# Layer 3's up-projection in 15 ktiles as two-by-two blocks with seven products

## The chip, the core and the metric

One NeuronCore of a Trainium2 chip runs one forward step of a four-layer model. The metric is the device time of one execution in microseconds. A core has TensorE (matmuls, PE in the profile, with its weight loads as PEld), VectorE (DVE), ScalarE (ACT), GpSimd (POOL) and SyncE (SP), which run side by side from queues of their own. TensorE multiplies a stationary tile of 128x128 with up to 512 moving columns and writes to PSUM; the other operands lie in SBUF.

## The reference, cut to what matters

Each of the four layers is a token mixer and then a gated ConvFFN. There are 640 tokens (512 of a sample, 128 of a prompt), a width of 1024, and 2816 = 22 x 128 hidden features.

```python
def _conv_ffn(h, w_up, conv_w, conv_b, w_down):
    a, b = jnp.split(h @ w_up, 2, axis=-1)
    ap = jnp.pad(a, ((0, 0), (1, 1), (0, 0)))
    a = ap[:, :-2] * conv_w[0] + ap[:, 1:-1] * conv_w[1] + ap[:, 2:] * conv_w[2] + conv_b
    return (jax.nn.gelu(a) * b) @ w_down
...
        f = (ffn_w_up[i], ffn_conv_w[i], ffn_conv_b[i], ffn_w_down[i])
        x_p = _layer_norm(ALPHA * x_p + m_p[5] * _conv_ffn(h_p, *f), ln_g[i, 1], ln_b[i, 1])
        x_s = _layer_norm(ALPHA * x_s + m_s[5] * _conv_ffn(h_s, *f), ln_g[i, 1], ln_b[i, 1])
```

## The kernel before

Activations are feature-major: a ktile is 128 features on the partitions by 640 tokens. Every float32 operand of a product is split into a high part that TensorE takes as it is and a low part (the rest), and `mm3` (lines 172 to 177) adds three matmuls: high by high, high by low, low by high. `unit` (line 157) loads a piece of weights into a `raw` slot (4 of them), copies the high part on ScalarE (line 163) and subtracts on VectorE (line 164) into a slot of the pool `hlp` (tag `hl`, 6 slots of 8 KB per partition). `split` (line 167) does the same for an activation, which lies in one of 16 slots of `actp`.

The tokens are worked on in two parts, half A of 256 and half B of 384 columns (`HALVES`). In `ffn` (line 560) `up(j)` makes hidden ktile j: two weight units (the convolved branch a and the gate b), each times both halves, over 8 input ktiles; then `ffn_a` copies a into a padded buffer `ap`, and `ffn_g` applies the convolution (lines 512, 514), the gelu (516) and the gate (518, 519) and splits the result. `down` multiplies a chunk of hidden ktiles with the down weights, 8 output ktiles by two halves, and `evac` (436) adds them to x. A chunk's down-projection is issued after the first ktile of the next chunk. The first six ktiles of layer 3 have half A done ahead (`ffn_pre`) and half B in `skew`. Before, the chunks are ktiles 0 to 6, 7 to 13 and 14 to 21; the last one goes through `project`, in which a LayerNorm's steps are issued at fixed positions among the products (`LN_A`).

In layers 0 to 2 VectorE also makes the next layer's modulation (`mod_dve`, line 273) beside the FFN; in layer 3 nothing of that is left, and `bg` does nothing. A scheduler orders each engine's instructions ahead of the run, by program order among those whose operands and slots it expects to be there; each engine then runs its queue in that order and waits at semaphores.

Of the kernel before, what the change touches and what calls it, by code (L numbers as in the profile page):

```python
# [16 lines left out]
D = 1024  # L17
# [16 lines left out]
# half 0 runs ahead of half 1, and 2 of 3 (in front of the pooling, which reads neighbours)  # L34
HALVES = ((0, 256), (256, 640), (0, 384), (384, 640))
HW = 384
# (start, stop, group) with group 0 = sample, 1 = prompt
SEGS = (((0, 256, 0),), ((256, 512, 0), (512, 640, 1)), ((0, 384, 0),), ((384, 512, 0), (512, 640, 1)))
# ktiles of the FFN between its down-projections
FFN_CHUNKS = ((0, 7), (7, 14), (14, 22))  # L40
SKEW = {None: 7, 2: 6, 3: 6, 1: 6, 0: 6}
# units of a projection's weights that half B finds from half A
KEEP = {None: 4, (0, 0): 3, (1, 1): 5, (3, 1): 5, (1, 0): 3, (3, 0): 5}
# layer 0's modulation, blocks of 512 features, in plain float32
MOD32 = (2, 0)
# SKEW ktiles of the FFN run half A ahead of half B, 2 SKEW units of weights: the last SPLIT of them in split parts
# (SPLIT_AHEAD units ahead of their use), of which half B finds the last KEPT; h is split SPLIT_H units from the end
# [17 lines left out]
BAND_KIND = (0, 1, 1, 2, 3)
# tiles of the LN; ktiles that are centred ahead (of the two LNs of a half, and of the last)
# [10 lines left out]
# columns of the packed per-partition vectors  # L77
# [33 lines left out]
class Kern:  # L111
    def __init__(self, ctx, tc, a):
# [4 lines left out]
        self.actp = P("actp", 16)  # L117
        self.hlp = P("hlp", 6)
# [38 lines left out]
    def unit(self, src, shape, e=None):  # L157
        """A piece of weights, split exactly into two float32r parts."""
        nc = self.nc
        r = self.raw(shape)  # L160
        self.load(r, src)
        hl = self.hlp.tile([128, 2] + list(shape[1:]), F32R, tag="hl", name=self.nm("hl"))
        nc.scalar.copy(hl[:, 0], r)  # L163
        (e or nc.vector).tensor_sub(hl[:, 1], r, hl[:, 0])  # L164
        return hl

    def split(self, dst, src, e=None):
        """dst [:, 0] + [:, 1] = src exactly."""
        self.nc.scalar.copy(dst[:, 0], src)  # L169
        (e or self.nc.vector).tensor_sub(dst[:, 1], src, dst[:, 0])  # L170

    def mm3(self, out, lhs, rhs, start, stop):
        """out += lhs^T rhs with (hi, lo) pairs of operands."""
        t = self.nc.tensor
        t.matmul(out, lhs[0], rhs[0], start=start, stop=False)  # L175
        t.matmul(out, lhs[0], rhs[1], start=False, stop=False)  # L176
        t.matmul(out, lhs[1], rhs[0], start=False, stop=stop)  # L177
# [4 lines left out]
    def table(self, f, x):  # L182
        """Has the tables of an activation function loaded ahead of its use, once x is there."""
        self.nc.scalar.activation(self.small("tab", [128, 1]), x.bitcast(F32), f)

    def consts(self):
# [24 lines left out]
        self.cbc = cp.tile([128, 2, D], F32, name="cbc")  # L211
        self.aps = [cp.tile([128, T + 3], F32, name=f"ap{i}") for i in range(2)]
        self.bgq, self.bgf = [], 0.0
        # modulation [part, chunk, ktile, group]
        self.mod = [cp.tile([128, 6, NK, 2], F32, name=f"mod{i}") for i in range(DEPTH)]

    def cond_rows(self):
        """silu(cond) along the free dimension, on every partition."""
# [1181 lines left out]
```

## Time and profile before

| | |
|---|---|
| time, median of 3 runs | 2803.09 us (2801.15 to 2807.25) |
| span of the profiled execution | 2805.7 us |
| layer 3's FFN behind its first LN, to the end | about 2345 to 2806 us |
| TensorE busy | 2749.6 us (98%) |
| VectorE, ScalarE, GpSimd busy | 1973.0, 1240.0, 407.5 us |

The span runs from the first to the last instruction of one profiled execution, whose own time is that span of 2805.7 us; the three runs are timed without a profile. Busy time of TensorE is modelled at its end, since matmuls overlap: a matmul's duration is longer than its distance to the next one. An idle engine costs time only where another one waits for it.

### The profile page before, as it was taken

What the parts mean: (1) busy time and instruction counts of PE and PEld (TensorE: products, weight loads), DVE (VectorE), ACT (ScalarE), POOL (GpSimd) and SP (SyncE); (2) the same over time, 40 slices, a digit from 0 to 9 for tenths busy, and PEclk for the clock granted to TensorE, in tenths of its full rate; (3) what the DMA queues carried; (4) which work ended last, traced back from release to release, by engine and by line L of the source; (5) the groups of instructions that cost most, each with busy time, mean ns of one, the idle gap of its engine ahead of it and who ended that gap; (6) DMA issues with size and microseconds to landing.
All of it is one profiled execution on the core that took longest, in us unless ns stands there. A gap on an engine that the chain in (4) does not pass through costs nothing.

```text
span 2805.7 us, 46039 instructions
## 1 busy us (share of the span) xinstructions
PE 2749.6 (98%) x17826; PEld 2636.0 (94%) x17826; DVE 1973.0 (70%) x4263; ACT 1240.0 (44%) x2286; POOL 407.5 (15%) x417
## 2 busy tenths in 40 slices
PE   7999999999999999999999999999999999999998
PEld 4799999999989999999978999999799999999998
DVE  6879977857697887777587878775756558534344
ACT  5656232336496752323367423234532248423233
POOL 1250000024303300000442000005100042000003
PEclk9999999999999999999989999999999999999999
DMA  7735644432402445455104554542422224322221
GB/s 241 259 109 163 198 154 149 156 121 80 134 22 83 136 153 158 149 157 153 56 35 150 151 165 151 158 136 80 161 65 91 68 62 152 97 82 68 83 75 54
DMA packets 99932, 344.70 MB, mean 123 GB/s; under 512 B 11392, under 2 KB 14080, under 8 KB 99584
## 3 DMA queue, kind: packets, MB, share of 16 engines
q1 hardware_dynamic: 99712, 341.74, 38.7%
q8 instruction: 141, 2.31, 0.3%
q14 instruction: 79, 0.65, 0.1%
HBM read 336.19 MB, written 2.88 MB: 121 GB/s over the span
## 4 chain that ended last, share of the span: by engine, by line
PE 88%; DVE 5%; issue 2%; ACT 2%; DMA 2%; POOL 1%; POOLq 0%; ACTq 0%; SPq 0%; DVEq 0%
PE mm L175 26%; PE mm L176 26%; PE mm L177 26%; PE mm L487 2%; PE st L352 1%; PE mm L1157 1%; DVE hl L164 1%; DVE tmp L339 1%; DMA raw<-in_wmod 1%; PE mm L1247 1%; PE bc L372 1%; DVE lnt L383 1%; DVE act L170 0%; PE mm L1072 0%; DMA raw<-in_wup 0%
## 5 line engine op out<-in xcount | busy, mean ns | idle before, releaser
L177 PE MATMUL mm<-act,hl 128*128 128x384 f32 (+2 forms) x4928 | 1528.5, 310 | 3.2 <-DVE hl L164 3.2
L175 PE MATMUL mm<-act,hl 128*128 128x384 f32 (+2 forms) x4928 | 1531.5, 311 | 0.0
L176 PE MATMUL mm<-act,hl 128*128 128x384 f32 (+2 forms) x4928 | 1528.6, 310 | 1.2 <-POOL act L418 1.2
L177 PEld LDWEIGHTS mm<-act,hl 128*128 128x128 f32 x4928 | 935.1, 190 | 5.0 <-DVE hl L164 4.4
L176 PEld LDWEIGHTS mm<-act,hl 128*128 128x128 f32 x4928 | 935.9, 190 | 3.7 <-POOL act L418 1.8
L175 PEld LDWEIGHTS mm<-act,hl 128*128 128x128 f32 x4928 | 935.2, 190 | 3.2 <-ACT hl L163 0.6
L163 ACT CAST hl<-raw 128x1024 fp32r<-128x1024 f32 (+1 forms) x433 | 444.1, 1030 | 625.9 <-PE mm L177 560.1
L164 DVE TENSOR_TENSOR hl<-raw,hl 128x1024 fp32r<-128x1024 f32 (+1 forms) x428 | 526.0, 1231 | 67.4 <-ACT hl L163 65.1
L283 DVE SCALAR_TENSOR_TENSOR bc<-raw,cbc 128x512 f32<-128x512 f32 x608 | 406.2, 719 | 130.3 <-DMA raw<-in_wmod 130.0
L436 DVE SCALAR_TENSOR_TENSOR x<-mm,mod,x 128x256 f32<-128x256 f32 (+2 forms) x408 | 166.0, 434 | 200.4 <-PE mm L177 199.8
L514 DVE SCALAR_TENSOR_TENSOR tmp<-ap,vecs,tmp 128x512 f32<-128x512 f32 x352 | 170.5, 547 | 147.6 <-ACT tmp L512 147.4
L333 POOL TENSOR_TENSOR tmp<-x,tmp 128x256 f32<-128x256 f32 (+1 forms) x180 | 178.0, 993 | 153.2 <-DVE x L436 109.0
L527 POOL MEMSET ap<- 128x1 f32 x24 | 2.1, 99 | 1188.4 <-DVE tmp L514 735.3
L502 ACT COPY ap<-mm 128x256 f32<-128x256 f32 x88 | 33.0, 375 | 265.2 <-PE mm L177 265.2
L333 POOL TENSOR_TENSOR tmp<-x 128x256 f32<-128x256 f32 (+1 forms) x30 | 30.7, 1024 | 733.3 <-DVE x L436 694.5
L383 DVE TENSOR_TENSOR lnt<-x,bc 128x256 f32<-128x256 f32 (+1 forms) x240 | 109.6, 479 | 14.9 <-PE bc L372 14.4
L332 ACT ACTIVATE lnt<-x 128x256 f32<-128x256 f32 (+1 forms) x112 | 51.2, 467 | 133.3 <-DVE x L436 130.9
L516 ACT ACTIVATE tmp<-tmp 128x640 f32<-128x640 f32 x88 | 65.2, 740 | 100.4 <-DVE tmp L514 100.4
L169 ACT CAST act<-tmp 128x640 fp32r<-128x640 f32 x117 | 84.9, 726 | 52.1 <-DVE tmp L519 31.8
L512 ACT ACTIVATE tmp<-ap,vecs 128x512 f32<-128x512 f32 (+1 forms) x176 | 106.4, 658 | 0.0
L339 DVE TENSOR_TENSOR tmp<-tmp,lnt 128x384 f32<-128x384 f32 (+1 forms) x126 | 93.7, 745 | 14.1 <-ACT lnt L332 12.6
L487 PE MATMUL mm<-h,raw 128*128 128x256 f32 x416 | 101.2, 399 | 1.8 <-DVE lnt L404 1.8
(209 smaller groups left out, 2684.1 us busy)
## 6 DMA issues: line engine op xcount, KB each, us to landing
raw<-in_wup SPq DMA_DIRECT2D x216, 512.0 KB, 3.5
raw<-in_wmod SPq DMA_DIRECT2D x184, 512.0 KB, 3.5
raw<-in_wdn SPq DMA_DIRECT2D x64, 448.0 KB, 3.4
raw<-in_wdn SPq DMA_DIRECT2D x46, 512.0 KB, 3.6
raw<-in_wgv SPq DMA_DIRECT2D x24, 512.0 KB, 4.1
raw<-in_wgo SPq DMA_DIRECT2D x19, 512.0 KB, 3.9
raw<-in_wqk SPq DMA_DIRECT2D x18, 512.0 KB, 3.5
raw<-in_wgu SPq DMA_DIRECT2D x16, 512.0 KB, 3.5
```

The source lines that it names most:

```text
L163: nc.scalar.copy(hl[:, 0], r)
L164: (e or nc.vector).tensor_sub(hl[:, 1], r, hl[:, 0])
L175: t.matmul(out, lhs[0], rhs[0], start=start, stop=False)
L176: t.matmul(out, lhs[0], rhs[1], start=False, stop=False)
L177: t.matmul(out, lhs[1], rhs[0], start=False, stop=stop)
L283: nc.vector.scalar_tensor_tensor(out=self.bc(), in0=r[:, sl], scalar=1.0, in1=self.cbc[:, g, sl], op0=ALU.mult, op1=ALU.mult, accum_out=ac ...
L333: nc.gpsimd.tensor_add(S.s[0], z, S.s[0] if n > 1 else S.first)
L339: (self.nc.gpsimd if S.pool else self.nc.vector).tensor_add(S.s[1], S.s[1], S.last)
L383: self.nc.vector.tensor_sub(t, self.x[:, k, a:b], MU)
L436: nc.vector.scalar_tensor_tensor(out=self.x[:, m, s0:s1], in0=ps[:, s0 - a:s1 - a], scalar=sc, in1=self.x[:, m, s0:s1], op0=ALU.mult, op1= ...
L487: self.nc.tensor.matmul(ps, w[:, k, :], h32[:, k, :], start=k == 0, stop=k == NK - 1)
L514: nc.vector.scalar_tensor_tensor(out=c[:, sl], in0=ap[:, o + i:o + i + n], scalar=cw(i), in1=c[:, sl], op0=ALU.mult, op1=ALU.add)
```

## The change

For ktiles 7 to 21 of layer 3, `up` is replaced by `up7`. The two weight tiles a and b, each cut into input ktiles 0 to 3 and 4 to 7, are a block matrix of two by two, and h, cut into the same input halves and two halves of 320 tokens, is another. Their product is made from seven block products in place of eight, from sums and differences of blocks. The sums of weights are made on VectorE for every ktile (`S`); the sums of h are made once, in `seven_pre`, in steps beside the first chunk's down-projection, some of them in place of blocks of h. The sums of products are made through copies of PSUM on ScalarE and additions on VectorE, while X and Z go on accumulating. The gate comes with its sign changed, so `ffn_g` gets a form with -1. The low part of the unsummed weights (`wA`) is made by a negated copy on ScalarE and a DMA from GpSimd that adds the raw weights to it.

Layer 3's chunks become 0 to 5, 6 to 10, 11 to 14 and 15 to 21. `actp` has 18 slots, `hlp` 7, of which the conditioning rows `cbc` hold one until layer 2's FFN is done; GpSimd's scratch for DMAs is set to 4096 bytes, which makes room for these. Comments were removed.

```diff
-FFN_CHUNKS = ((0, 7), (7, 14), (14, 22))
+FFN_CHUNKS = {None: ((0, 7), (7, 14), (14, 22)), 3: ((0, 6), (6, 11), (11, 15), (15, 22))}
+SEVEN = {None: NJ, 3: 7}
+HT = T // 2
...
-        self.actp = P("actp", 16)
-        self.hlp = P("hlp", 6)
+        self.actp = P("actp", 18)
+        self.hlp = P("hlp", 7)
...
+    def halves(self, hl, r, e=None, dma=False):
+        nc = self.nc
         nc.scalar.copy(hl[:, 0], r)
-        (e or nc.vector).tensor_sub(hl[:, 1], r, hl[:, 0])
-        return hl
+        if dma:
+            nc.scalar.activation(hl[:, 1], r, AF.Copy, scale=-1.0)
+            nc.gpsimd.dma_start(hl[:, 1].bitcast(F32), r, accum_op=ALU.add)
+        else:
+            (e or nc.vector).tensor_sub(hl[:, 1], r, hl[:, 0])
...
-        self.cbc = cp.tile([128, 2, D], F32, name="cbc")
+        self.cbc = self.hlp.tile([128, 2, D], F32, tag="hl", name="cbc")
...
-    def ffn_g(self, L, j, ap, bA, bB):
+    def ffn_g(self, L, j, ap, bA, bB, neg=False):
...
+        if neg:
+            c = self.tmp([128, T + 1])
+            nc.scalar.activation(c, ap[:, 0:T + 1], AF.Identity, scale=cw(0), bias=self.vec(V_CB + L * NJ + j))
+            for i in (1, 2):
+                nc.vector.scalar_tensor_tensor(out=c, in0=ap[:, i:i + T + 1], scalar=cw(i), in1=c, op0=ALU.mult, op1=ALU.add)
+            nc.scalar.activation(c, c, AF.Gelu_apprx_tanh)
+            g = self.tmp([128, T])
+            for x, y, ps in ((0, 0, bA), (HT, HT, bB[:, 0:512 - HT]), (512, 513, bB[:, 512 - HT:HT])):
+                w = ps.shape[1]
+                nc.vector.scalar_tensor_tensor(out=g[:, x:x + w], in0=ps, scalar=-1.0, in1=c[:, y:y + w],
+                                               op0=ALU.mult, op1=ALU.mult)
+            o = self.act()
+            self.split(o, g)
+            return o
...
                     self.evac(ps, L, 5, m, half)
                     self.bg(at(BG, L))
+                steps(beside, 1)
+
+        def seven_pre():
+            acts = [self.act([128, 2, 2, HT]) for _ in range(3)]
...
+            for k in range(4):
+                if k < 2:
+                    room = [acts[k][:, 0], acts[k][:, 1], acts[2][:, k]]
+                else:
+                    t = self.hlp.tile([128, 3, 2, HT], F32R, tag="hl", name=self.nm("op"))
+                    room = [t[:, i] for i in range(3)]
+                up, lo = fl(hs[k][:, :, :]), fl(hs[k + 4][:, :, :])
+                w, z = self.tmp([128, 2, HT]), self.tmp([128, 2, HT])
+                v.tensor_sub(w, up[:, :, A], up[:, :, B])
+                v.tensor_add(w[:, 0], w[:, 0], w[:, 1])
+                self.split(room[0], w[:, 0])
+                v.tensor_sub(z, lo[:, :, B], up[:, :, B])
+                v.tensor_add(z[:, 0], z[:, 0], z[:, 1])
+                self.split(room[1], z[:, 0])
+                yield
+                v.scalar_tensor_tensor(out=z[:, 0], in0=z[:, 0], scalar=-1.0, in1=up[:, 0, A], op0=ALU.mult, op1=ALU.subtract)
+                v.tensor_sub(z[:, 0], z[:, 0], up[:, 1, A])
+                self.split(room[2], z[:, 0])
+                v.scalar_tensor_tensor(out=z[:, 0], in0=z[:, 0], scalar=-1.0, in1=lo[:, 0, A], op0=ALU.mult, op1=ALU.subtract)
+                v.tensor_sub(z[:, 0], z[:, 0], lo[:, 1, A])
+                self.split(hs[k][:, :, B], z[:, 0])
...
+        def up7(j, ops):
+            v = nc.vector
+            ra, rb = self.raw_unit(a["wup"][L, 2 * j]), self.raw_unit(a["wup"][L, 2 * j + 1])
+            new = lambda n=8: self.hlp.tile([128, 2, n, 128], F32R, tag="hl", name=self.nm("hl"))
+            a1, a2, b1, b2 = ra[:, 0:4], ra[:, 4:8], rb[:, 0:4], rb[:, 4:8]
+            S = self.hlp.tile([128, 16, 128], F32, tag="hl", name=self.nm("sums"))
+            v.tensor_add(S[:, 4:8], b1, b2)
+            v.tensor_add(S[:, 0:4], a1, b1)
+            v.tensor_add(S[:, 8:12], a1, S[:, 4:8])
+            v.tensor_add(S[:, 12:16], a2, S[:, 8:12])
+            wA, wB, wC, wD = new(), new(), new(), new(4)
+            self.halves(wA, ra, dma=True)
+            self.halves(wB, S[:, 8:16])
+            self.halves(wC, S[:, 0:8])
+            self.halves(wD, b2)
+            X, Y, Z = self.mm([128, HT]), self.mm([128, HT]), self.bc([128, HT])
+            def prod(ps, w, k0, rhs, first):
+                for k in range(4):
+                    self.mm3(ps, (w[:, 0, k0 + k], w[:, 1, k0 + k]), rhs[k], first and k == 0, k == 3, not first)
+            def keep(ps):
+                t = self.small("lnt", [128, HT], LNT)
+                nc.scalar.copy(t, ps)
+                return t
+            ap = self.aps[j % 2]
+            prod(X, wA, 0, ops[0], True)
+            r1 = keep(X)
+            prod(Y, wA, 4, ops[1], True)
+            v.tensor_add(ap[:, 1:1 + HT], r1, Y)
+            prod(X, wB, 0, ops[2], False)
+            r2 = keep(X)
+            prod(Z, wC, 4, ops[3], True)
+            m5 = keep(Z)
+            prod(X, wC, 0, ops[4], False)
+            v.tensor_add(m5, m5, X)
+            prod(Z, wB, 4, ops[5], False)
+            v.tensor_add(ap[:, 1 + HT:513], r2[:, 0:512 - HT], Z[:, 0:512 - HT])
+            v.tensor_add(ap[:, 514:642], r2[:, 512 - HT:HT], Z[:, 512 - HT:HT])
+            prod(X, wD, 0, ops[6], False)
+            gs[j] = self.ffn_g(L, j, ap, X, m5, neg=True)
...
-        for ci, (k0, k1) in enumerate(FFN_CHUNKS):
+        for ci, (k0, k1) in enumerate(at(FFN_CHUNKS, L)):
...
-                up(j)
+                if j >= at(SEVEN, L):
+                    up7(j, ops)
+                else:
+                    up(j)
...
-                    down(*pend, False)
+                    pre7 = seven_pre() if j + 1 == at(SEVEN, L) else iter(())
+                    down(*pend, False, pre7)
+                    ops = next(pre7, ops)
...
-    nc = _bacc.Bacc("TRN2", target_bir_lowering=False, num_devices=1)
+    nc = _bacc.Bacc("TRN2", target_bir_lowering=False, num_devices=1,
+                    dynamic_dma_scratch_size=4096)
```

## Rows read from the trace of the kernel before

**Rows 1.** Page, parts 1 and 2: busy us by engine, granted clock by slices.
```profile
PE 2749.6 (98%) x17826; PEld 2636.0 (94%) x17826; DVE 1973.0 (70%) x4263; ACT 1240.0 (44%) x2286; POOL 407.5 (15%) x417
...
PEclk9999999999999999999989999999999999999999
```

**Rows 2.** Windows: length, then PE, PEld, DVE, ACT, POOL busy; clock, DMA share, GB/s.
```profile
2561.35:2575.42 14.07, 14.07 (x98) 14.07 (x97) 5.66 (x9) 5.15 (x10) 0.00 (x0) 1.00 0.24 67
...
2587.50:2636.00 48.50, 48.50 (x333) 48.50 (x332) 19.28 (x32) 7.96 (x10) 0.00 (x0) 1.00 0.27 88
```

**Rows 3.** TensorE's waits, 2345 us to the end: total us, times, longest.
```profile
PE mm L177 <- DVE hl L164: 1.7, 1, 1.7
PE bc L372 <- POOL lnv L360: 1.6, 2, 1.4
PE st L352 <- POOL tmp L333: 1.6, 1, 1.6
```

**Rows 4.** Timeline of TensorE in one ktile: start us, duration us, instruction.
```profile
2561.03 0.28 PE L177 MATMUL mm<-act,hl 128*128 128x256 f32 x1
2561.15 0.34 PE L175 MATMUL mm<-act,hl 128*128 128x384 f32 x1
...
2565.14 0.33 PE L177 MATMUL mm<-act,hl 128*128 128x384 f32 x1
2565.32 0.28 PE L175 MATMUL mm<-act,hl 128*128 128x256 f32 x1
...
2568.06 0.28 PE L177 MATMUL mm<-act,hl 128*128 128x256 f32 x1
```

**Rows 5.** Timeline of TensorE in layer 1's scores: first and last of six.
```profile
852.78 0.31 PE L175 MATMUL mm<-act,act 128*128 128x320 f32 x1
...
853.51 0.31 PE L177 MATMUL mm<-act,act 128*128 128x320 f32 x1
```

**Rows 6.** VectorE by form, 2410 to 2735 us: busy us, mean ns | idle before.
```profile
L164 DVE TENSOR_TENSOR hl<-raw,hl 128x1024 fp32r<-128x1024 f32 x33 | 40.4, 1223 | 9.4 <-ACT hl L163 9.4
L514 DVE SCALAR_TENSOR_TENSOR tmp<-ap,vecs,tmp 128x512 f32<-128x512 f32 x32 | 24.0, 749 | 86.9 <-ACT tmp L512 86.9
...
L170 DVE TENSOR_TENSOR act<-tmp,act 128x640 fp32r<-128x640 f32 x16 | 13.1, 819 | 0.0
L514 DVE SCALAR_TENSOR_TENSOR tmp<-ap,vecs,tmp 128x128 f32<-128x128 f32 x32 | 11.1, 347 | 0.0
```

**Rows 7.** Timeline of VectorE: one ktile's four convolution steps.
```profile
2566.80 1.94 DVE L514 SCALAR_TENSOR_TENSOR tmp<-ap,vecs,tmp 128x512 f32<-128x512 f32 x4 [5.52 <-ACT tmp L512]
```

**Rows 8.** ScalarE by form, the same stretch and columns as rows 6.
```profile
L163 ACT CAST hl<-raw 128x1024 fp32r<-128x1024 f32 x34 | 35.6, 1046 | 94.8 <-PE mm L177 94.8
...
L169 ACT CAST act<-tmp 128x640 fp32r<-128x640 f32 x16 | 11.6, 723 | 0.0
...
L502 ACT COPY ap<-mm 128x256 f32<-128x256 f32 x16 | 6.0, 374 | 60.6 <-PE mm L177 60.6
```

**Rows 9.** DMA issues, whole span: KB each, median us from issue to landing.
```profile
raw<-in_wup SPq DMA_DIRECT2D x216, 512.0 KB, 3.5
...
x<-in_xT SPq DMA_DIRECT2D x1, 2560.0 KB, 9.9
```

**Rows 10.** Timelines of VectorE and GpSimd in the last project.
```profile
2739.56 1.23 DVE L164 TENSOR_TENSOR hl<-raw,hl 128x1024 fp32r<-128x1024 f32 x1 [0.47 <-ACT hl L163]
...
2743.71 1.78 DVE L164 TENSOR_TENSOR hl<-raw,hl 128x1024 fp32r<-128x1024 f32 x1 [0.47 <-ACT hl L163]
...
2744.37 1.99 POOL L339 TENSOR_TENSOR tmp<-tmp,lnt 128x384 f32<-128x384 f32 x1
```

**Rows 11.** TensorE's waits on split weights, whole span: total us, times, longest.
```profile
PE mm L177 <- DVE hl L164: 3.2, 4, 1.7
PE mm L176 <- DVE hl L164: 2.8, 2, 1.7
```

**Rows 12.** Timeline of ScalarE behind the product of rows 4's first line.
```profile
2561.35 0.38 ACT L500 COPY ap<-mm 128x256 f32<-128x256 f32 x1 [1.30 <-PE mm L177]
```

More of the change, by code (lines that the diff above doesn't have):

```diff
@@ L155, in load, with unit @@
         self.nc.sync.dma_start(dst, src)
-    def unit(self, src, shape, e=None):
+    def unit(self, src, shape, e=None, dma=False):
         nc = self.nc
@@ L162, in unit @@
         hl = self.hlp.tile([128, 2] + list(shape[1:]), F32R, tag="hl", name=self.nm("hl"))
+        self.halves(hl, r, e, dma)
+        return hl
+    def halves(self, hl, r, e=None, dma=False):
+        nc = self.nc
         nc.scalar.copy(hl[:, 0], r)
-        (e or nc.vector).tensor_sub(hl[:, 1], r, hl[:, 0])
-        return hl
+        if dma:
[3 more added lines that the diff above has]
+            (e or nc.vector).tensor_sub(hl[:, 1], r, hl[:, 0])
     def split(self, dst, src, e=None):
@@ L170, in split, with mm3 @@
         (e or self.nc.vector).tensor_sub(dst[:, 1], src, dst[:, 0])
-    def mm3(self, out, lhs, rhs, start, stop):
+    def mm3(self, out, lhs, rhs, start, stop, on=False):
         t = self.nc.tensor
-        t.matmul(out, lhs[0], rhs[0], start=start, stop=False)
-        t.matmul(out, lhs[0], rhs[1], start=False, stop=False)
-        t.matmul(out, lhs[1], rhs[0], start=False, stop=stop)
+        t.matmul(out, lhs[0], rhs[0], start=start, stop=False, skip_group_check=on)
+        t.matmul(out, lhs[0], rhs[1], start=False, stop=False, skip_group_check=on)
+        t.matmul(out, lhs[1], rhs[0], start=False, stop=stop, skip_group_check=on)
     def vec(self, col, n=1):
@@ L210, in consts @@
         nc.vector.tensor_sub(self.condr[:, :, 2:4], self.cond, self.condr[:, :, 0:2])
-        self.cbc = cp.tile([128, 2, D], F32, name="cbc")
+        self.cbc = self.hlp.tile([128, 2, D], F32, tag="hl", name="cbc")
+        nc.vector.memset(self.cbc[:, 0, 0:2], 0.0)
         self.aps = [cp.tile([128, T + 3], F32, name=f"ap{i}") for i in range(2)]
@@ L598, in down_unit, with down @@
             return f
-        def down(k0, k1, last):
+        def down(k0, k1, last, beside=iter(())):
             us = down_unit(k0, k1)
@@ L614, in down @@
                     self.bg(at(BG, L))
+                steps(beside, 1)
+        def seven_pre():
+            acts = [self.act([128, 2, 2, HT]) for _ in range(3)]
+            n1, n2, t3 = [], [], []
+            v = nc.vector
+            fl = lambda x: x.bitcast(F32)
+            A, B = slice(0, HT), slice(HT, T)
+            for k in range(4):
[19 more added lines that the diff above has]
+                self.split(hs[k][:, :, B], z[:, 0])
+                for o, r in zip((n1, t3, n2), room):
+                    o.append(r)
+                yield
+            b = lambda k, sl: (hs[k][:, 0, sl], hs[k][:, 1, sl])
+            pair = lambda t: (t[:, 0], t[:, 1])
+            yield ([b(k, slice(0, HT)) for k in range(4)], [b(k + 4, slice(0, HT)) for k in range(4)],
+                   [pair(t) for t in n2], [pair(t) for t in n1], [pair(t) for t in t3],
+                   [b(k + 4, slice(HT, T)) for k in range(4)], [b(k, slice(HT, T)) for k in range(4)])
@@ new lines, in up7 @@
+        def up7(j, ops):
+            v = nc.vector
+            ra, rb = self.raw_unit(a["wup"][L, 2 * j]), self.raw_unit(a["wup"][L, 2 * j + 1])
[24 more added lines that the diff above has]
+            v.tensor_add(ap[:, 1:1 + HT], r1, Y)
+            self.bg(at(BG, L))
+            prod(X, wB, 0, ops[2], False)
+            r2 = keep(X)
+            prod(Z, wC, 4, ops[3], True)
+            m5 = keep(Z)
+            self.bg(at(BG, L))
+            prod(X, wC, 0, ops[4], False)
[3 more added lines that the diff above has]
+            v.tensor_add(ap[:, 514:642], r2[:, 512 - HT:HT], Z[:, 512 - HT:HT])
+            self.bg(at(BG, L))
+            prod(X, wD, 0, ops[6], False)
+            self.bg(at(BG, L))
+            gs[j] = self.ffn_g(L, j, ap, X, m5, neg=True)
@@ L616, in ffn @@
         if L == 0:
             self.bgq.append(self.mod_dve(0, 40, 48))
+        ops = None
         pend = None
-        for ci, (k0, k1) in enumerate(FFN_CHUNKS):
+        for ci, (k0, k1) in enumerate(at(FFN_CHUNKS, L)):
             if ci == 0:
```

## The prediction

> **What bounds the kernel now.** I read the page's first two parts first. TensorE is busy 98% of the span, VectorE 70%, ScalarE 44%, and the granted clock stands at 9 tenths or more in nearly every slice [rows 1]. Then a table by stretches of layer 3's FFN: one ktile of the up-projection takes 14.07 us, a chunk of seven ktiles of the down-projection fills the 48.5 us shown beside it, and in both TensorE is busy for the whole stretch at clock 1.00, the full level of 2.4 GHz, while VectorE works 5.66 of 14.07 us and ScalarE 5.15 [rows 2]. Third, the list of TensorE's waits from 2345 us on: one wait of 1.7 us for split weights at the start, and the LN's waits near the end; the steady part has none [rows 3]. So in this stage time is the number of matmuls times their spacing, and an instruction on another engine costs nothing until it makes TensorE wait.
>
> **What is removed.** Spacing, start to start, is what counts, not the duration of 0.28 or 0.33 us, since matmuls overlap. From the first to the last of 24 matmuls of 384 columns are 3.99 us, of 256 columns 2.74 us; divided by 23 that is 0.173 and 0.119 us [rows 4]. An up-projection ktile has two weight tiles by two parts of the tokens by 8 input ktiles by 3 matmuls: 48 of each width, 48 x 0.173 + 48 x 0.119 = 14.0 us, which is the measured 14.07. The new ktile has seven products of 4 input ktiles by 3 matmuls, 84 in all, with 320 columns each. That width exists in layer 1's scores, where six starts in a row span 0.73 us, 0.146 each [rows 5]; 84 x 0.1465 = 12.31 us. So 1.76 us are saved per ktile, and for 15 ktiles **26.4 us**. The other chunk borders change neither number nor width of the down-projection's matmuls. Chunks of 6, 5, 4 and 7 in place of 7, 7 and 8 add eight weight units and 16 accumulations with their evacuation; TensorE pays nothing for them, and VectorE is idle for over half of a down stretch (19.28 of 48.5 us busy) [rows 2].
>
> **VectorE per new ktile.** From the rows of the stretch by form [rows 6], between whose sizes the cost grows by 1.05 ns a column: four sums of weights at 512 columns, 0.685 us each by the line through 640 (0.819) and 1024 (1.223), 2.74; three low parts of 1024, 1024 and 512 columns, 3.13; four sums of products, 1.6; two convolution steps of 641 columns, 1.77; three gate products, 1.31; the low part of g, 0.82. Together 11.4 us in 17 instructions. Back to back they overlap: four convolution steps whose durations add up to 2.19 us take 1.94 us [rows 6, 7], 0.085 us less per instruction, so 17 of them occupy about 9.9 of 12.31 us. That fits, at 81%, but the slack of the old ktile is gone. ScalarE: four copies and one negated copy of weights (4.5 x 1.05 us), three copies of products (0.43 each), convolution start, gelu and the copy of g, about 8.4 us [rows 8]; that fits easily.
>
> **Slots.** There are 7 slots for split weights; two hold operands from now on, so five are left, and one ktile uses five (sums, A, B, C, D). Ktile j+1 finds its slots as j lets go of them. With t = 0 at the first product of j and 1.76 us a product: A is free at 3.5, C at 8.8, B at 10.5, D at 12.3. New B takes C's slot and is wanted 15.8 after t = 0, new C takes B's and is wanted at 17.6; a cast (1.05), a subtraction (1.22) and some waiting leave 3 to 4 us. New D has 8 us. Only new A is tight: slot free at 3.7, casts and the copies that ScalarE owes in between (A's high part, the copy of the preceding g, a product's copy, the negated copy: 1.05 + 0.72 + 0.43 + 1.1) end at 7.0, then GpSimd issues the accumulating DMA, and the third matmul at 12.6 wants its result. So the DMA is hidden if issue to landing takes up to **5.5 us**.
>
> **The accumulating DMA** is an operation that the trace doesn't show. A plain load of the same 512 KB lands in 3.5 us and one of 2560 KB in 9.9 [rows 9]; so each 512 KB beyond the first costs 1.6 us. An accumulation must read its target too, twice the bytes: 3.5 + 1.6 = 5.1 us, nearest to the first row, and I take that: hidden, **0 us**. The bounds are 3.5 (no more than a load) and 9.9 us, by the far row; at the latter 4.4 us would be missing in each of the 12 ktiles that follow directly on another one (those at 7, 12 and 16 follow on a down-projection, whose units of 3.5 to 5 us leave longer leads), or 53 us.
>
> The Trainium skill (DMA: Bandwidth & Descriptors, "Anatomy of one DMA — SWDGE (gpsimd) path") gives about 2.0 us plus bytes at 436 GB/s for a DMA issued by GpSimd, an estimate of 3.2 us for one pass of 512 KB and 4.4 us with the target read as well. By it the DMA is hidden with a us to spare and the sum stays the same; no run here shows such a DMA yet.
>
> **Handoffs within a ktile.** X and Z gather several products, so the third, fifth, sixth and seventh product must each wait until a copy or a sum has read the bank. One product of 1.76 us covers each. In today's rows ScalarE starts 0.04 us after a product's end, which lies 0.16 us behind the next one's start [rows 4, 12]. Behind a running cast of 1.05 us a copy of 0.43 is done at 1.7 us: just inside. On VectorE a running subtraction of 1.22 us and a sum of 0.48 give 1.8 to 1.9 us, 0.1 too late. Bounds for 60 handoffs: 0, and 0.1 each, 6 us; I take **2 us**, since only one handoff of four is VectorE's and it rarely meets a fresh subtraction.
>
> **The operands, made beside the first down-projection.** Per input ktile 12 VectorE instructions (two of 640 columns, ten of 320), 6.6 us, for four 26.4; the eight weight units of 6 ktiles and the evacuations add 8 x 2.2 us. That makes 44 us, some 37 with the overlap above, in 8 x 5.27 = 42 us of TensorE work. It fits if nothing else comes; the first new ktile's sums and low parts come too (6 us). Bounds 0 and 6 us; I take **2 us**. The steps are queued on VectorE ahead of later weight splits, so those would be what TensorE waits for.
>
> **The tail.** The last project has 7 instead of 8 ktiles, so half B's 22.9 us become 20.0 and LN steps at fixed positions come earlier. There TensorE already waits 1.6 us for GpSimd's sums and up to 1.4 for its power [rows 3]. Position 8 comes 0.36 us earlier, position 23 another 0.67. Bounds 0 and 1.5; I take **1 us**.
>
> **Layers 0 to 2** get 18 instead of 16 activation slots; the six weight slots are the same ones until layer 2 is done, since the conditioning rows occupy the seventh. TensorE's waits on split weights come to 3.2 and 2.8 us over the whole span [rows 11]; about half of that could go or come again: I take 0, bounds -3 and +3.
>
> **Sum.** -26.4 + 0 + 2 + 2 + 0 + 1 = -21.4 us. The profiled execution has a span of 2805.7 us, 2.6 us over the median of 2803.09 and inside the runs' spread, so differences carry over: 2803.1 - 21.4 = **2781.7 us**. With all costs at their low ends 2803.1 - 26.4 - 3 = 2774; with the highs except the DMA's, 2793.
>
> **Rivals.**
> *The DMA paces (slower).* If the landing takes L us over 5.5, each of 12 ktiles waits L - 5.5. With 5 us of other costs the gain is gone at L = 5.5 + 21.4/12 = 7.3 us, which lies between the two load rows. At 8.5 us: 2803.1 - 26.4 + 36 + 5 = 2818 us. For it: descriptors made by GpSimd in software and a read-modify-write, neither of which is in the trace; DMA rows of this stretch already show two loads per ktile. Against it: the queues are a quarter busy there [rows 2]. Chance 0.14.
>
> *VectorE paces.* While GpSimd reads SBUF, a VectorE subtraction of two SBUF operands took 1.78 instead of 1.23 us [rows 10]. If the eight sums and low parts of a ktile (6.7 us) all ran at that rate, 3.0 us would be added: 9.9 becomes 12.9, 0.6 us over the pace in 15 ktiles, 9 us: 2791 us; with the overlap gone too, 14.4 us, 2803.1 - 26.4 + 31 + 5 = 2813. Against it: GpSimd has no arithmetic in this stretch [rows 2], only the DMA's issue. Chance 0.10.
> The Trainium skill (SBUF — State Buffer, "Who interferes with whom") says that a VectorE instruction with two SBUF inputs contends only with GpSimd instructions that read SBUF, not with those that only write. Rows 10 agree on the first half; by the second this rival would cost nothing.
>
> *It doesn't do what it says.* The issue order is fixed ahead of the run. If the copies of products stand one cast too far back, a handoff takes 0.16 + 0.04 + 2.1 + 0.43 = 2.7 us, 1 us too long; one such handoff per ktile costs 15 us (2797 us with the other terms), two cost 30 (2812). Against it: in today's stretch copies start 0.04 us after their product [rows 12]. Chance 0.10.
>
> **Numbers.** The forecast, 2774 to 2793, has 0.66. Of the rivals, the DMA's 0.14 is nearly all slower (0.12, and 0.02 about the same); VectorE's 0.10 splits into 0.06 faster, 0.03 same, 0.01 slower; the order's into 0.02, 0.03 and 0.05. About 0.2%, 5.6 us, is what a measurement of this kernel can tell from no change. So faster 0.74, same 0.08, slower 0.18. The range reaches from 2773 to 2806: it takes in the likeliest case and the milder half of the rivals, and leaves out little below and 0.17 above.
>
> **What would show it.** Right: starts of 320-column matmuls 0.146 us apart, ktiles 12.3 us apart, TensorE busy over the whole of the stretch. Each term has its place: a wait of the third matmul of a ktile on a GpSimd DMA is the first rival; a wait at the first matmul of the third, fifth, sixth or seventh product on ScalarE or VectorE is the handoff; VectorE over 95% busy is the second rival; waits in the first down stretch are the operands'. The forecast is wrong if the landing exceeds 7 us, or if TensorE's idle time in the stretch adds up to more than 20 us.

## The result and the profile after

| | before | changed |
|---|---|---|
| time, median of 4 runs each | 2804.27 us | 2783.05 us (2779.24 to 2784.92) |
| ratio, 95% interval | | 0.9922 [0.9908, 0.9936] |
| span of the profiled execution | 2805.7 us | 2779.9 us |

The change makes the kernel 0.8% faster. A second comparison of the same kernel, run with the experiments below, gave 0.9925 [0.9912, 0.9937].

The page of the changed kernel, where it answers to rows 1: TensorE has 180 matmuls fewer (15 ktiles, 84 in place of 96) and 26.8 us less to do, VectorE and ScalarE have more, and there is a DMA queue that GpSimd feeds (the last line, from the list of DMA issues: KB each, median us from issue to landing).

```profile
span 2779.9 us, 46012 instructions
...
PE 2722.8 (98%) x17646; PEld 2607.5 (94%) x17646; DVE 2063.7 (74%) x4464; ACT 1289.5 (46%) x2340; POOL 419.3 (15%) x432
...
hl<-raw POOLq DMA_DIRECT2D x15, 512.0 KB, 4.5
```

The windows that answer to rows 2 (same columns): all five ktiles of the first run of new ktiles, then two of them alone. Each lasts 12.32 us instead of 14.07, TensorE is busy without a break at clock 1.00, and VectorE works 10.1 us, ScalarE 8.1 us of it.

```profile
2466.53:2528.12 61.59, 61.59 (x422) 61.59 (x421) 45.87 (x78) 37.38 (x52) 3.47 (x4) 1.00 0.43 110
2491.16:2503.48 12.32, 12.32 (x87) 12.32 (x85) 10.10 (x18) 8.10 (x12) 0.86 (x1) 1.00 0.48 129
2503.48:2515.80 12.32, 12.32 (x87) 12.32 (x85) 10.11 (x18) 8.09 (x12) 0.86 (x1) 1.00 0.41 97
```

The list of TensorE's waits from ktile 6 to the end, as in rows 3 (total us, times, longest). In 15 new ktiles and three down-projections nothing is waited for; what is left are the LN's waits, 1.9 where 1.6 was, and one of 0.2 us in the last project.

```profile
PE st L366 <- POOL tmp L347: 1.9, 1, 1.9
PE bc L386 <- POOL lnv L374: 1.4, 1, 1.4
PE bc L386 <- DVE lnv L370: 0.3, 1, 0.3
PE mm L187 <- ACT act L181: 0.2, 1, 0.2
```

Layer 3's part can be measured by itself. ScalarE's copy of ktile 6's first product is the last landmark that both kernels share. First the line of before, then that of the changed kernel, from ScalarE's timelines:

```profile
2413.71 0.38 ACT L500 COPY ap<-mm 128x256 f32<-128x256 f32 x1 [1.29 <-PE mm L177]
```

```profile
2413.39 0.38 ACT L514 COPY ap<-mm 128x256 f32<-128x256 f32 x1 [1.40 <-PE mm L189]
```

From there to the end of the span are 2805.7 - 2413.7 = 392.0 us before and 2779.9 - 2413.4 = 366.5 us after. I call this the **stage**; it became **25.5 us** shorter, and it is compared in every experiment, since the same stage of the changed kernel run again came to 366.4 us, within 0.1.

### The profile page after: what moved, and what is told of

It reads as the page before. It is cut to its first block, busy times and chain, and to the rows that moved or that the text cites. A ratio compares the mean times of both kernels' runs of the same rounds, so it can differ in the third digit from the quotient of the medians.

```text
span 2779.9 us, 46012 instructions
## 1 busy us (share of the span) xinstructions
PE 2722.8 (98%) x17646; PEld 2607.5 (94%) x17646; DVE 2063.7 (74%) x4464; ACT 1289.5 (46%) x2340; POOL 419.3 (15%) x432
## 4 chain that ended last, share of the span: by engine, by line
PE 87%; DVE 5%; ACT 3%; DMA 2%; issue 2%; POOL 1%; SPq 0%; POOLq 0%; ACTq 0%; DVEq 0%
PE mm L187 26%; PE mm L188 26%; PE mm L189 26%; PE mm L501 2%; PE st L366 1%; DVE hl L177 1%; DVE tmp L353 1%; DMA raw<-in_wmod 1%; ACT x L410 1%; PE mm L1370 1%; PE bc L188 1%; PE bc L189 1%; PE bc L187 1%; ACT hl L172 1%; DVE lnt L409 1%
## 5 line engine op out<-in xcount | busy, mean ns | idle before, releaser
L187 PE MATMUL mm<-act,hl 128*128 128x384 f32 (+3 forms) x4688 | 1455.7, 311 | 0.9 <-ACT act L431 0.7
L189 PE MATMUL mm<-act,hl 128*128 128x384 f32 (+3 forms) x4688 | 1453.2, 310 | 2.3 <-DVE hl L177 2.1
L188 PE MATMUL mm<-act,hl 128*128 128x384 f32 (+3 forms) x4688 | 1453.1, 310 | 2.4 <-POOL act L432 1.5
L188 PEld LDWEIGHTS mm<-act,hl 128*128 128x128 f32 x4688 | 888.3, 189 | 5.0 <-POOL act L432 2.5
L187 PEld LDWEIGHTS mm<-act,hl 128*128 128x128 f32 x4688 | 887.5, 189 | 4.5 <-ACT act L431 0.9
L189 PEld LDWEIGHTS mm<-act,hl 128*128 128x128 f32 x4688 | 887.5, 189 | 4.1 <-DVE hl L177 3.7
L172 ACT CAST hl<-raw 128x1024 fp32r<-128x1024 f32 (+4 forms) x441 | 438.9, 1001 | 517.9 <-PE mm L189 427.7
L177 DVE TENSOR_TENSOR hl<-raw,hl 128x1024 fp32r<-128x1024 f32 (+4 forms) x421 | 499.6, 1190 | 55.4 <-ACT hl L172 52.9
L450 DVE SCALAR_TENSOR_TENSOR x<-mm,mod,x 128x256 f32<-128x256 f32 (+2 forms) x432 | 175.9, 435 | 159.9 <-PE mm L189 159.1
L543 DVE SCALAR_TENSOR_TENSOR tmp<-ap,vecs,tmp 128x512 f32<-128x512 f32 (+1 forms) x292 | 141.6, 547 | 59.9 <-ACT tmp L541 59.6
L181 ACT CAST act<-tmp 128x640 fp32r<-128x640 f32 (+1 forms) x127 | 89.2, 705 | 68.5 <-DVE tmp L548 36.5
L182 DVE TENSOR_TENSOR act<-tmp,act 128x640 fp32r<-128x640 f32 (+1 forms) x127 | 100.7, 794 | 7.9 <-ACT act L181 7.7
L353 DVE TENSOR_TENSOR tmp<-tmp,lnt 128x384 f32<-128x384 f32 (+1 forms) x126 | 93.5, 744 | 13.8 <-ACT lnt L346 12.3
L545 ACT ACTIVATE tmp<-tmp 128x640 f32<-128x640 f32 x73 | 54.1, 741 | 105.5 <-DVE tmp L543 105.4
L410 ACT ACTIVATE x<-lnt,vecs 128x256 f32<-128x256 f32 (+1 forms) x128 | 82.4, 649 | 27.6 <-DVE lnt L409 26.8
```

Source lines behind the costliest of these rows:

```text
L187: t.matmul(out, lhs[0], rhs[0], start=start, stop=False, skip_group_check=on)
L188: t.matmul(out, lhs[0], rhs[1], start=False, stop=False, skip_group_check=on)
L189: t.matmul(out, lhs[1], rhs[0], start=False, stop=stop, skip_group_check=on)
L353: (self.nc.gpsimd if S.pool else self.nc.vector).tensor_add(S.s[1], S.s[1], S.last)
L410: nc.scalar.activation(z, t, AF.Identity, scale=scale, bias=bias)
L450: nc.vector.scalar_tensor_tensor(out=self.x[:, m, s0:s1], in0=ps[:, s0 - a:s1 - a], scalar=sc, in1=self.x[:, m, s0:s1], op0=ALU.mult, op1= ...
```

## The experiments

All of them start from the changed kernel. "Stage" is the stretch above, 366.5 us in the changed kernel. In two_dmas, six_slots, keep_thrice and vector_over the scheduler also orders TensorE's matmuls otherwise: in 12, 12, 12 and 9 of the 15 new ktiles a few matmuls of a later product stand ahead of those that wait. In the other kernels with 15 new ktiles their order is that of the changed kernel.

| kernel | time, us | ratio to before, 95% interval | stage, us |
|---|---|---|---|
| again | 2783.61 | 0.9925 [0.9912, 0.9937] | 366.4 |
| no_seven | 2804.53 | 0.9998 [0.9990, 1.0007] | 392.1 |
| ten_ktiles | 2790.70 | 0.9948 [0.9933, 0.9963] | 375.2 |
| two_dmas | 2868.14 | 1.0231 [1.0215, 1.0246] | 449.0 |
| low_on_vector | 2782.15 | 0.9921 [0.9907, 0.9934] | 366.7 |
| six_slots | 2826.83 | 1.0081 [1.0064, 1.0098] | 412.7 |
| keep_thrice | 2785.99 | 0.9932 [0.9917, 0.9947] | 372.8 |
| ops_after | 2782.23 | 0.9918 [0.9901, 0.9934] | 366.4 |
| vector_full | 2781.79 | 0.9916 [0.9899, 0.9932] | 367.4 |
| vector_over | 2788.29 | 0.9937 [0.9923, 0.9952] | 374.3 |
| sum_on_gpsimd | 2789.24 | 0.9943 [0.9928, 0.9958] | 373.7 |

### Is it the number of matmuls? (again, no_seven, ten_ktiles)

The changed kernel once more, for a narrower interval and a second trace:

> The changed kernel as it is, to narrow the gain. Hidden-work theory (all that the change adds lies beside TensorE's matmuls, the gain is 15 ktiles times 14.07 - 12.32 = 26.2 us, less about 0.7 us at the end): 25 us under the kernel before, a ratio of 0.991. If the gain is really the 21.2 us of the first medians, 4 us are lost somewhere that the profiled execution didn't show: ratio 0.9925.

The chunks, slots and scratch of the change, but no ktile with seven products:

```diff
-SEVEN = {None: NJ, 3: 7}
+SEVEN = {None: NJ}
```

> Ktiles 7 to 21 go through the old up-projection again; chunk borders, 18 and 7 slots and the conditioning rows' place stay as changed. Hidden-work theory: the seven products are the whole gain, so this kernel has the old time, span 2805 us within 3, ktiles 14.07 us apart. Rival (the slots and chunks bring part of the gain, by fewer waits in layers 0 to 3): span 2800 us or less.

Seven products in 10 instead of 15 ktiles:

```diff
-SEVEN = {None: NJ, 3: 7}
+SEVEN = {None: NJ, 3: 12}
```

> Only ktiles 12 to 21 are made by seven products; the operands are then made beside the second down-projection (5 ktiles, 8 x 4.39 = 35 us of TensorE, against some 36 us of VectorE work). Hidden-work theory: the gain is 1.75 us per ktile, so five ktiles fewer cost 8.8 us, span 2789 us, plus 0 to 6 us where the operands don't fit beside the shorter chunk. Rival (a fixed part of the gain, not proportional to the ktiles): span 2780 to 2784 us.

Without the seven products the kernel is at the time of before (0.9998), and the stage at 392.1 us: the other chunk borders, the 18 activation slots, the seventh weight slot and the smaller scratch are together worth nothing that the measurement can tell. With 10 such ktiles the stage is 375.2 us, 8.7 us more than with 15: 8.7 / 5 = 1.74 us a ktile, where the windows give 14.07 - 12.32 = 1.75. So the gain is linear in the number of ktiles.

### Is the accumulating DMA hidden, and how far? (two_dmas, low_on_vector, six_slots)

A second accumulating DMA behind the first. The copy is taken times -2, and what is too much is added back, so the result stays the low part:

```diff
-            nc.scalar.activation(hl[:, 1], r, AF.Copy, scale=-1.0)
+            nc.scalar.activation(hl[:, 1], r, AF.Copy, scale=-2.0)
             nc.gpsimd.dma_start(hl[:, 1].bitcast(F32), r, accum_op=ALU.add)
+            nc.gpsimd.dma_start(hl[:, 1].bitcast(F32), hl[:, 0].bitcast(F32), accum_op=ALU.add)
```

> The copy is scaled by -2, and a second accumulating DMA of the same size, chained behind the first, adds the high part: the same low part, twice the landing. DMA theory (A's low part is due at the third matmul of the next ktile, 2.1 us after today's landing): the second landing comes 4.5 us later, TensorE waits about 2.5 us at the third matmul of 12 ktiles, 30 us, span 2810 us; none at ktiles 7, 12 and 16, which follow on a down-projection. Rival (there is much more room than 2.1 us): span 2780 us.

The kernel became slower than before. The stage grew by 82.5 us. GpSimd's timeline of one ktile, and then the page's rows on the two DMAs (KB each, median us to landing):

```profile
2468.97 0.87 POOL L175 DMA_DIRECT2D hl<-raw  x1 [13.31 <-ACT hl L174]
2474.34 0.86 POOL L176 DMA_DIRECT2D hl<-hl  x1 [4.50 <-DMA hl<-raw]
```

```profile
hl<-raw POOLq DMA_DIRECT2D x15, 512.0 KB, 4.6
hl<-hl POOLq DMA_DIRECT2D x15, 512.0 KB, 6.4
```

The second is issued 5.4 us after the first and lands 6.4 us later: 11.8 us from the first issue. TensorE's waits, and then the windows of the same ktile (columns as in rows 2): the wait, the matmuls behind it, and what follows.

```profile
PE mm L190 <- DMA hl<-hl: 54.3, 14, 5.5
```

```profile
2475.56:2480.74 5.18, 0.31 (x4) 0.05 (x2) 3.85 (x6) 0.62 (x2) 0.00 (x0) 0.92 0.98 274
2480.74:2486.77 6.03, 6.03 (x23) 6.03 (x23) 0.99 (x4) 1.06 (x2) 0.00 (x0) 0.50 0.05 20
2486.77:2495.72 8.95, 8.95 (x63) 8.95 (x62) 5.53 (x9) 6.24 (x8) 1.72 (x2) 1.00 0.40 78
```

It is the third matmul of the ktile, in the order of the program, that waits, as the DMA rival said. Of the ktiles behind a down-projection, which I expected to be spared, only 7 was; 12 waited 0.5 and 16 waited 2.9 us. The cost has two parts: the waits, 54.3 us in 14 ktiles, and the time behind them. In the second window 23 matmuls take 6.03 us, 0.262 each where 0.1465 is the rule, at a granted clock of 0.50, which is the lower of the two levels (1.2 GHz); ahead of it two starts lie 5.2 us apart, so TensorE had stood for 5.0 us. Over the stage the slower starts make up the rest of the 82.5 us, some 28 us. It is more than was expected by both: the second landing takes 6.4 us where the first takes 4.6, and the waits have this price behind them.

The low part of `wA` on VectorE, as for the other weights, without negated copy and DMA:

```diff
-            self.halves(wA, ra, dma=True)
+            self.halves(wA, ra)
```

> The low part of the unsummed weights is a VectorE subtraction instead of ScalarE's negated copy and GpSimd's DMA. VectorE goes from 10.10 to about 11.3 of 12.32 us per ktile. Hidden-work theory: TensorE still never waits, span 2780 us within 2, so the DMA buys nothing here. Rival (VectorE paces before it is full, since its sums of products come behind subtractions): 0.3 to 1 us per ktile, span 2785 to 2795 us, waits at the first matmul of the seventh product or on ap.

2782.15 us, with no wait in the new ktiles. The window of a ktile shows VectorE at 11.13 of 12.32 us and ScalarE at 7.24:

```profile
2491.16:2503.48 12.32, 12.32 (x87) 12.32 (x86) 11.13 (x20) 7.24 (x11) 0.00 (x0) 1.00 0.22 70
```

So the DMA costs nothing here, and it brings nothing either: VectorE would have had room for that subtraction. The edit also takes a copy of 1.06 us off ScalarE, which matters in the next section.

Six slots instead of seven for split weights, the conditioning rows in a place of their own again:

```diff
-        self.hlp = P("hlp", 7)
+        self.hlp = P("hlp", 6)
-        self.cbc = self.hlp.tile([128, 2, D], F32, tag="hl", name="cbc")
+        self.cbc = cp.tile([128, 2, D], F32, name="cbc")
```

> Six slots for split weights and the conditioning rows in a place of their own, so layers 0 to 2 have what they had; a new ktile finds four slots instead of five. Slot theory: the sums take A's slot and new A has to wait for C's, freed at 8.8 instead of 3.5 us of a ktile; its DMA lands 5.3 us later, 3.2 us after it is due, in 12 ktiles: 38 us, span 2818 us, with the wait at the third matmul. Rival (the slots aren't the limit): 2780 us.

The stage is 46.2 us longer, and the kernel slower than before. TensorE's waits:

```profile
PE mm L189 <- DMA hl<-raw: 19.1, 12, 1.8
PE bc L187 <- ACT hl L172: 8.4, 12, 0.9
```

Twelve ktiles, those that follow directly on another one, wait for both, 27.5 us. The wait for ScalarE is that of matmuls which the scheduler put ahead of the one that waits for the DMA. In ktile 8 that one, the third in the order of the program, starts at 2482.04 us, where 2478.72 was due: 3.3 us late, and 3.2 had been worked out from the slot. The rest of the 46.2 us are starts further apart behind the waits: four of the twelve ktiles last 15.1 us, and eight, which have a stretch of matmuls 0.27 us apart, 16.6 to 16.9. So the slot is what the change could not do without; it could do without the DMA (low_on_vector).

### How much room have the handoffs? (keep_thrice, vector_full, vector_over, sum_on_gpsimd)

ScalarE copies each product three times:

```diff
-                nc.scalar.copy(t, ps)
+                for _ in range(3):
+                    nc.scalar.copy(t, ps)
```

> Each of the three copies of products on ScalarE is made three times in a row. Cover theory (the copy r2 ends 0.33 us before the fifth product wants its bank, at 2497.87 against 2498.20 us in the profile; two more copies take 0.66 us): a wait of 0.3 us at the fifth product of each ktile and none at the others, 4 to 5 us, span 2785 us. Rival 1 (one product covers far more than that): no wait, 2780 us. Rival 2 (ScalarE, at 10.5 of 12.3 us, falls behind and delays the weights too): 1 us per ktile, 2795 us.

The stage is 6.3 us longer. TensorE stands before the fifth product, 0.42 to 0.46 us in six ktiles and less in the others, and before the third product too, 0.12 to 0.18 us in eight, where I had expected none; behind each wait a start or two come 0.1 us late. TensorE's waits on these copies, as the list has them (it counts from the modelled end of the matmul ahead), and the wait before one fifth product, from its timeline:

```profile
PE mm L187 <- ACT lnt L711: 1.7, 6, 0.3
```

```profile
2496.88 0.41 PE L187 MATMUL mm<-act,hl 128*128 128x320 f32 x1 [0.26 <-ACT lnt L711]
```

The changed kernel's ScalarE timeline, and the start of the fifth product from TensorE's, show why it is the fifth:

```profile
2494.14 0.74 ACT L528 ACTIVATE tmp<-tmp 128x641 f32<-128x641 f32 x1 [0.55 <-DVE tmp L527]
2494.92 1.05 ACT L172 CAST hl<-raw 128x1024 fp32r<-128x1024 f32 x1
2495.88 1.06 ACT L174 ACTIVATE hl<-raw 128x1024 fp32r<-128x1024 f32 x1
2496.84 0.71 ACT L181 CAST act<-tmp 128x640 fp32r<-128x640 f32 x1
2497.45 0.42 ACT L710 COPY lnt<-mm 128x320 f32<-128x320 f32 x1
2498.40 0.43 ACT L710 COPY lnt<-bc 128x320 f32<-128x320 f32 x1 [0.53 <-PE bc L189]
```

```profile
2498.20 0.31 PE L187 MATMUL mm<-act,hl 128*128 128x320 f32 x1
```

The gelu of the preceding ktile, three copies of operands (one of them the negated one) and then the copy of X, without a pause; it ends at 2497.87, and the fifth product, which goes on in the same bank, starts at 2498.20. That leaves 0.33 us, and two more copies of 0.32 us don't fit. (With a copy of Z that the scheduler put in between they are three more; four matmuls of the next ktile, put ahead of the fifth product, cover part of it.)

VectorE subtracts `wA`'s low part two or three times (n = 2 or 3 in place of copy and DMA):

```diff
-        if dma:
-            nc.scalar.activation(hl[:, 1], r, AF.Copy, scale=-1.0)
-            nc.gpsimd.dma_start(hl[:, 1].bitcast(F32), r, accum_op=ALU.add)
-        else:
-            (e or nc.vector).tensor_sub(hl[:, 1], r, hl[:, 0])
+        for _ in range(n if dma else 1):
+            (e or nc.vector).tensor_sub(hl[:, 1], r, hl[:, 0])
```

> The negated copy and the accumulating DMA of wA are replaced by VectorE's subtraction, and that subtraction is issued twice, so that VectorE has one instruction of 1.22 us more than in low_on_vector, where it was busy 11.13 of a ktile's 12.32 us. 11.13 + 1.22 = 12.35 us, just at TensorE's pace. Theory (a handoff or a split is late only when VectorE has more work than a ktile lasts; what is queued in front of it costs nothing below that): the time of low_on_vector, 2782 us, plus up to 3 us, with VectorE nearly 100% busy in the ktiles. Rival (the sums of products are already close to late, as the 0.1 us per handoff of the prediction says, and VectorE at the full makes each of the three a subtraction later): 0.5 to 1 us in each of 15 ktiles, 2790 to 2797 us, with TensorE's waits on VectorE at the third, sixth or seventh product.

> As vector_full, but wA's subtraction is issued three times: 11.13 + 2 x 1.22 = 13.57 us of VectorE work per ktile of 12.32 us. Theory (VectorE's queue then sets the pace): 1.25 us are missing per ktile; in the 12 ktiles that follow directly on another one these are waits, 15 us, and the ktiles behind a down-projection start with a lead that takes up part of it: 2782 + 10 to 19 = 2792 to 2801 us, and more if the waits become long enough to bring the matmuls' spacing down with the granted clock, as in the runs with a second DMA and with six slots. Rival (VectorE is not what ends last even there, since a ktile has slack between its splits and the next ktile's first use): under 2787 us.

With n = 2, the first fence, VectorE is busy 12.26 of 12.32 us and the time is 2781.79 us: no wait longer than 0.1 us in the new ktiles. With n = 3, the second, the time is 6.5 us more and the stage 6.9. There are just two waits on these subtractions, each in the fifth ktile of a run of ktiles:

```profile
2491.16:2503.48 12.32, 12.32 (x86) 12.32 (x85) 12.26 (x20) 7.24 (x10) 0.00 (x0) 1.00 0.26 86
```

```profile
PE mm L186 <- DVE hl L174: 5.3, 2, 2.7
```

Here my expectation of 10 to 19 us was too high: the lead that VectorE has behind a down-projection pays for 1.25 us a ktile over four ktiles, not over one, so the chunk of four never waits. Neither kernel tests VectorE alone: with the DMA the negated copy on ScalarE is gone as well, so the copy of X ends 0.94 us ahead of the fifth product in both low_on_vector and vector_full, not 0.33. What a full VectorE costs with that copy in place is not shown.

The first sum of weights on GpSimd:

```diff
-            v.tensor_add(S[:, 4:8], b1, b2)
+            nc.gpsimd.tensor_add(S[:, 4:8], b1, b2)
```

> The first of the four sums of weights (128x512, 0.69 us on VectorE) is made by GpSimd, about 2.65 us by its 1.99 us for 384 columns; all else is as in the changed kernel, VectorE busy 10.1 of 12.32 us. By rows 10 a VectorE subtraction with two SBUF operands beside GpSimd's arithmetic takes 1.78 instead of 1.23 us. Theory (VectorE has 2.2 us to spare per ktile): VectorE loses 0.69 and gains some 0.6 to 1.2 us where it meets GpSimd, the chain of sums and low parts starts 2 us later, and all of that stays hidden: 2783 us within 3. Rival (VectorE paces, or GpSimd's queue delays the accumulating DMA that stands behind the sum): a wait of 0.5 to 2 us per ktile, 2790 to 2813 us.

The theory failed: VectorE has nearly as much room as before (10.3 of 12.3 us busy), and still the stage is 7.2 us longer. TensorE's waits, then GpSimd's and VectorE's timelines in one ktile:

```profile
PE mm L187 <- ACT lnt L710: 4.9, 9, 0.6
```

```profile
2494.06 1.86 POOL L692 TENSOR_TENSOR sums<-raw 128x512 f32<-128x512 f32 x1 [6.08 <-DVE hl L177]
```

```profile
2494.68 1.79 DVE L177 TENSOR_TENSOR hl<-raw,hl 128x512 fp32r<-128x512 f32 x1
2496.39 0.87 DVE L527 SCALAR_TENSOR_TENSOR tmp<-ap,vecs,tmp 128x641 f32<-128x641 f32 x1
```

Beside GpSimd's sum the subtraction of 512 columns takes 1.79 instead of 0.68 us, 1.1 more. The convolution step behind it, the gelu, the three copies and the copy of X come later, the last by 1.0 us; 0.33 were to spare, so some 0.7 us are missing, and the trace has gaps of 0.71 to 0.73 us before the fifth product in eight ktiles and 0.56 in a ninth, 0.1 us more behind each. Nine times 0.8 is the 7.2 us. The order of TensorE's matmuls is the changed kernel's here.

### Where are the operands best made? (ops_after)

All steps of `seven_pre` are issued behind the down-projection instead of among its products:

```diff
-                steps(beside, 1)
...
-                    ops = next(pre7, ops)
+                    for got in pre7:
+                        ops = got or ops
```

> The operand steps are written behind the whole first down-projection instead of one step behind each of its eight products. If the place in the program decides: 26 us of VectorE work lie between the down-projection and the first new ktile, some 20 us of waiting, span 2800 us. If the scheduler moves steps up as soon as their operands are there, into VectorE's idle time beside the down-projection: span 2780 to 2785 us.

Stage 366.4, time 2782.23 us: no difference. In its trace the VectorE instructions of these steps start between 2424.8 and 2457.8 us, beside the down-projection, which lasts until 2469.5 (2421.9 to 2455.6 us and until 2466.5 in the changed kernel): the scheduler moved them up. The place in the program is not what hides this work.

## Why the prediction was right, and where it was not

**The matmuls** carried the result, and the step held: 12.32 us a ktile where 84 x 0.1465 = 12.31 was worked out, 26.25 us in all for 26.4. Spacing read at 320 columns in another layer [rows 5], at the same granted clock, was valid here.

**VectorE and ScalarE**: 10.1 us for about 9.9, 8.1 for 8.4. Taking 0.085 us off per back-to-back instruction [rows 6, 7] was right; the plain sum of durations, 11.4, would have been too much.

**Slots and DMA.** The negated copy ends at 2496.94, 5.8 us after the ktile's first product (7.0 was worked out), GpSimd issues at 2497.23 and the DMA lands 4.5 us later, at 2501.7; the next ktile's third matmul starts at 2503.77. About 2 us are to spare, and nothing waits.

```profile
2497.23 0.86 POOL L175 DMA_DIRECT2D hl<-raw  x1 [11.45 <-ACT hl L174]
```

The forecast of 5.1 us was 0.6 too high, between bounds of 3.5 and 9.9. The Trainium skill (DMA: Bandwidth & Descriptors, "Anatomy of one DMA — SWDGE (gpsimd) path") gave an estimate of 4.4 us with the target read as well and 3.2 without; the 4.5 us measured agree with the first. The DMA rival's mechanism was real: with 11.8 us to the second landing and 6.5 us from issue to use, 5.3 us are missing, and in two_dmas that matmul starts 5.2 us late. Only its price was too low, since the matmuls behind a long wait start further apart.

**Handoffs**: 2 us were put in, 0 are in the trace. The step named the wrong engine. It feared VectorE's sum behind a fresh subtraction; VectorE stood idle for 1.59 us before that sum in the changed kernel:

```profile
2500.23 0.49 DVE L724 TENSOR_TENSOR lnt<-lnt,mm 128x320 f32<-128x320 f32 x1 [1.59 <-PE mm L189]
```

The tight one is ScalarE's copy ahead of the fifth product, with 0.33 us. There, keep_thrice and sum_on_gpsimd show what the order rival would have cost: 0.4 to 0.8 us in a ktile.

**VectorE rival**: not in this kernel, but its cause exists. With one copy less on ScalarE, VectorE's whole room had to be used up and more (vector_over) before TensorE waited for it. GpSimd's arithmetic does slow VectorE's subtraction, as rows 10 let expect, and by more: 0.68 became 1.79. While GpSimd only issues the DMA (from 2497.23), VectorE's sum and subtraction keep their durations:

```profile
2497.21 0.69 DVE L695 TENSOR_TENSOR sums<-raw,sums 128x512 f32<-128x512 f32 x1
2497.82 0.82 DVE L182 TENSOR_TENSOR act<-tmp,act 128x640 fp32r<-128x640 f32 x1
```

The Trainium skill (SBUF — State Buffer, "Who interferes with whom") has it that VectorE with two SBUF inputs contends only with GpSimd instructions that read SBUF; both lines agree, the sum on GpSimd with a slowing, the DMA's issue with none.

**Operands**: 2 us were put in, 0 were lost. In the stretch from ktile 6 to the first new ktile VectorE is busy 41.98 of 53.10 us and TensorE all of it. I had set some 37 us of work, and 6 for the first new ktile, against 42 us of TensorE. The room was larger: the first step of the operands starts at 2421.9 us, while ktile 6 is still running, and the stretch has 11 us of that ktile ahead of the down-projection. The 2 us stood for a queueing that didn't happen.

```profile
2413.40:2466.50 53.10, 53.10 (x360) 53.10 (x359) 41.98 (x87) 17.10 (x31) 1.05 (x1) 1.00 0.22 61
```

**Tail**: 26.25 - 25.5 = 0.75 us were lost in the stage; 0.3 of it is the longer LN wait and 0.2 the new wait in the last project; 1 us was put in.

**The sum came out right for a partly wrong reason.** The stage gained 25.5 us, not the 21.4 of the sum, since handoffs and operands cost nothing. The medians, however, differ by 2804.27 - 2783.05 = 21.2 us only. That the sum met them is luck in part: what two terms did not cost was lost ahead of ktile 6, where I had put 0 for layers 0 to 2 (bounds -3 and 3).

The two profiled executions don't show this loss: the landmark stands at 2413.7 us before and at 2413.4 in the changed kernel. But they are not median runs. A run's time is 1.7 us longer than its span (2781.62 us for 2779.9 in the changed kernel), so the 2805.7 us of before stand for a time of some 2807.4, 3 us over the median, and the changed kernel's lies 1.4 us under its own; the prediction set before's span beside the median of the times as if they were one measure. If the stage lasts as long in every run as in the kept traces (366.4 to 366.5 us in after, again and ops_after, 392.0 and 392.1 in before and no_seven), the time ahead of the landmark is 2411.1 us in the mean of 33 runs of before (2407 to 2417), 2410.6 in 11 of no_seven and 2414.7 in 9 of the changed kernel (2411 to 2418). So some 3 to 4 us are lost there with the seven products, though up to the landmark every engine's order is the same as in no_seven. Why stays open.

One thing that moves the landmark can be read from the traces. At about 700 us TensorE waits 1.7 us in all of them; behind it the granted clock falls to the lower level in some and not in others. The windows 690 to 712 us of before and of no_seven (columns as in rows 2):

```profile
690.00:712.00 22.00, 20.28 (x120) 18.63 (x120) 13.19 (x28) 15.66 (x35) 5.01 (x5) 0.92 0.23 73
```

```profile
690.00:712.00 22.00, 20.28 (x130) 19.14 (x129) 13.64 (x30) 16.53 (x37) 5.02 (x5) 1.00 0.24 73
```

A stretch of 1000 matmuls around it (the 4000th to the 5000th of the trace) takes 164.0 to 164.5 us in the seven traces with the fall and 162.4 to 163.0 in the six without. Over all profiled executions the landmark lies between 2409.8 (two_dmas) and 2416.3 us (ops_after). Both before and the changed kernel have this fall in their traces, so it is not shown to be what the seven products lose.

## What to carry to other kernels

Where TensorE never waits, count matmuls, take their spacing (not their duration) from any row of the same width at the same granted clock, and ask of every added instruction only whether it is done in time. Spare time is a property of a chain, not of an engine: VectorE could take 2.2 us of work more at no cost where the work stood behind that chain and ScalarE had a copy less to make (vector_full), while a delay of 1.1 us at one of its instructions in the chain reached TensorE through ScalarE's queue, in which only 0.33 us were to spare. A slot more can decide over such a change: with six the kernel was slower than before.

## What the runs showed of the hardware

- A DMA from GpSimd that adds 512 KB of SBUF to 512 KB of SBUF landed in 4.5 us (median of 15); a plain load of that size takes 3.5 [rows 9]. A second one directly behind it took 6.4 us; in that ktile's wait the DMA engines were 98% busy, with the loads of the ktiles to come among their work.
- A wait of TensorE can cost more than its length, and not the same each time. After 5.0 us of standing (two_dmas), 23 matmuls of 320 columns started 0.262 us apart at a granted clock of 0.50. After 2.8 us (vector_over) nine did in one ktile, and in the other a single start, 0.25 us, was late; after 0.7 us (sum_on_gpsimd) there was one such start.
- At one and the same wait of 1.7 us, near 700 us, the granted clock fell in seven executions and stayed in six; the fall was worth about 1.5 us.
- GpSimd's sum of 512 columns from SBUF took 1.86 us, and a VectorE subtraction of 512 columns beside it 1.79 instead of 0.68 us.
